# Stacked score products, q and k one step ahead, and row-wise sums of squares in a two-layer hybrid encoder

## The chip, the cores and the metric

The kernel runs on one core of one Trainium2 chip. The metric is the device time of one execution in microseconds (us), as the median of several runs. A profiled execution gives the trace from which every row below comes; its own time and its span (first to last instruction) stand in the table further down.

## The reference, cut to what matters

Two layers with 512 tokens of width 1024. In each layer one projection of x feeds three branches: a bidirectional state-space scan (SSD), a differential attention with rotary positions, and a cross-attention into 256 memory tokens. Sigmoid gates merge the branches, an output projection and a layer norm follow. The change lies in the differential attention:

```python
q = _apply_rope(dq.reshape(Bsz, S, 8, 2, 64), cos, sin)     # 8 heads, 2 maps each, 64 wide
k = _apply_rope(dk.reshape(Bsz, S, 8, 2, 64), cos, sin)
s = einsum('bqhcd,bkhcd->bhcqk', q, k) * 64 ** -0.5
p = softmax(s)
w = p[:, :, 0] - lam * p[:, :, 1]
o = einsum('bhqk,bkhe->bqhe', w, v)
o = _rmsnorm(o, diff_norm_w) * (1 - lambda_init)           # over the 128 columns of a head
y_diff = o * silu(dg)
```

Everything is float32 at the boundary.

## The kernel before, in words

**Precision.** Nearly all products are made of single-pass float32r matmuls on a high part and a low part. `split(h, l, x)` (L93) writes the high part with ScalarE and the rest with VectorE; `mm3` (L105) adds the products low*high, high*low and high*high in one PSUM bank. A few products are plain float32, among them the transposes and the heads' sums of squares.

**Weights and units.** `emit` (L131) runs through a plan of jobs. Each unit of weights (128x1024, 512 KB) is loaded into `wr` by SyncE's queue (two buffers), split into `wh` and `wl` (three buffers each), two units ahead of its use. All DMAs of the kernel are issued on SyncE's queue, in one order. A projection of one unit (`proj`, `proj2`) is 24 matmuls of 512 columns into a bank of the pool `pj` (three banks).

**Order.** The program's scheduler orders each engine's instructions by priority and by its own estimate of times; in the differential attention TensorE's order is written by hand (`manual_schedule`), and other work may be put between. Pools: `pm` four PSUM banks (scores, values), `pt` a single bank (transposes, sums), `pj` three.

**The differential attention (`diff`).** A step (L966) is one unit's projection in two halves, with jobs ahead of the first half and between the halves. For head h the units are `rope(h + 1, "q")`, `rope(h + 1, "k")` and two of gates' or values' parts, so a head takes four steps and the 32 query blocks of 128 rows are numbered s = 0 to 31. `rope` (L819) takes the projection to SBUF (`rx`), lets four small DMAs swap its 32-row groups into `rsw`, multiplies by cosine and sine, and splits the sum into two tiles `q0`, `q1` (or `k0`, `k1`). The head's first map lies in partitions 0 to 63, the second in 64 to 127. Step s issues `scores(s + 1)` first; between the halves come `values` (on even steps) and `turn(s)`, the transposes of a block's weights. `scores` (L873) makes six matmuls of 64 rows, maps alternating, into two banks:

```python
for n, (a, b) in enumerate(((ql, kh), (qh, kl), (qh, kh))):
    for c in range(2):
        rows = slice(64 * c, 64 * c + 64)
        self.mm(pss[c], a[rows, qs], b[rows, :], n == 0, n == 2)
```

then for each map a minimum (`fmx`, VectorE) and an exponential (`fpp`, ScalarE). `values(h, 1)` (L907) squares the head's output into a tile `fth`; `sums(h)` (L921), one step later, contracts it with a column of ones, four float32 products of one column each into `pt`, and ScalarE copies 128x4 numbers to `ss`. `norm` (L927) turns `ss` into the heads' factors, in a chain of small VectorE operations: once for heads 0 to 6 behind step 29, once for head 7 behind step 33. For the first seven heads `spread` transposes the factors, stores them, and `fin(h)` loads them broadcast; for head 7 `last` spreads them with TensorE in step 34. `fin(h)` multiplies and splits into the tiles `dy0`, `dy1`, from which the branch's output projection starts.

**Ahead gates.** `AHEAD` (L40) names gate projections that are made between the parts of the SSD, stored to DRAM and loaded again where they are used; the keys are (group, part) of the SSD, the values (branch, row of 128 columns). The gates of branch 1 that are not ahead are the last units of the differential attention.

Of the kernel before, what the change touches and what calls it, by code (L numbers as in the profile page):

```python
# [15 lines left out]
ALU = mybir.AluOpType  # L16
# [16 lines left out]

PCW, PCB, PNW, PGB, PDN, PLG, PLB, PDS, NP_ = 0, 120, 144, 160, 184, 185, 193, 201, 217

CID, CTF, CTB, CON, CMK, CINV, CSG, NCST = 0, 128, 256, 384, 512, 768, 769, 770

AHEAD = {(0, 1): [(2, 0)], (0, 2): [(2, 1)], (0, 3): [(2, 2)], (1, 0): [(2, 3)], (1, 2): [(2, 4)],  # L40
         (2, 0): [(2, 5)], (2, 2): [(2, 6)], (3, 0): [(2, 7)], (3, 2): [(1, 0)]}

# [7 lines left out]
def bc(ap, shape):  # L52
    return ap.broadcast_to(shape)


class Net:
# [736 lines left out]
    def diff(self, l):  # L793
# [3 lines left out]
        def begin():  # L797
            self.df_ctx = ExitStack()
            fp = self.fp = self.df_ctx.enter_context(self.tc.tile_pool(name="diffp", bufs=2, reuse_waits="tile"))
            self.dy = [self.t(fp, [P, KC, S], f"dy{i}", F32R, bufs=1) for i in range(2)]  # L800
            lt = self.t(fp, [P, S], "ro", bufs=1)
            lq = lt[:, :256].rearrange("p (i e) -> p i e", i=4)
            nc.sync.dma_start(out=lq, in_=self.a["lam"][l:l + 1].broadcast_to([P, 4, 64]))
            lp = lt[:, 256:384].rearrange("p (i e) -> p i e", i=2)
            lv = lq.rearrange("p (i j) e -> p i j e", j=2)
            self.tt(lp, lv[:, :, 0, :], lv[:, :, 1, :], ALU.mult)
            ls = self.t(fp, [P, 2], "ls", bufs=1)
            nc.vector.reduce_sum(out=ls, in_=lp, axis=AX.X)
            self.act(ls, ls, AF.Exp)
            self.nlam = self.t(fp, [P, 1], "nlam", bufs=1)  # L810
            self.tt(self.nlam, ls[:, 1:2], ls[:, 0:1], ALU.subtract)
            self.ts(self.nlam, self.nlam, -lam0, ALU.add)
            self.dnw = self.t(fp, [P, 1], "dnw", bufs=1)
            self.ts(self.dnw, self.par[:, PDN:PDN + 1], 0.5 * (1.0 - lam0), ALU.mult)
            self.qk, self.v = {}, {}
            self.sdy = self.t(fp, [P, KC, S], "sdy", bufs=1)
            self.s0, self.ss = (self.t(fp, [P, 4 * KC], f"fs{i}", bufs=1) for i in range(2))

        def rope(h, nm):  # L819
            def f(wh, wl):  # L820
                fp = self.fp
                ps = yield from self.proj2(wh, wl)
                x = self.t(fp, [P, S], "rx")

                self.act(x, ps, scale=-0.125 if nm == "q" else 1.0)
                sw = self.t(fp, [P, S], "rsw")
                for i in range(4):
                    nc.sync.dma_start(out=sw[32 * i:32 * i + 32], in_=x[32 * (i ^ 1):32 * (i ^ 1) + 32])
                self.tt(x, x, self.cos, ALU.mult)
                self.tt(sw, sw, self.sin, ALU.mult)  # L830
                self.tt(x, x, sw, ALU.add)

                self.qk[h, nm] = [self.t(fp, [P, S], f"{nm}{i}", F32R) for i in range(2)]
                self.split(*self.qk[h, nm], x)
            return f, (l, (UQ if nm == "q" else UK) + h)

        def vpart(h):
# [35 lines left out]
        def scores(s):  # L873
            h, qc = divmod(s, 4)
            fp = self.fp
            (qh, ql), (kh, kl) = self.qk[h, "q"], self.qk[h, "k"]
            qs = slice(qc * P, (qc + 1) * P)
            mx = self.t(fp, [P, 2], "fmx")
            sm = self.t(fp, [P, 2], "fsm")
            pp = self.pp[s] = self.t(fp, [P, 2, S], "fpp")  # L880
            s0 = self.s0[:, s:s + 1]

            pss = [self.bank(self.pm, "pm") for _ in range(2)]
            for n, (a, b) in enumerate(((ql, kh), (qh, kl), (qh, kh))):
                for c in range(2):
                    rows = slice(64 * c, 64 * c + 64)
                    self.mm(pss[c], a[rows, qs], b[rows, :], n == 0, n == 2)
            for c, ps in enumerate(pss):
                nc.vector.tensor_reduce(out=mx[:, c:c + 1], in_=ps, axis=AX.X, op=ALU.min)  # L889
                self.act(pp[:, c, :], ps, AF.Exp, scale=-1.0, bias=mx[:, c:c + 1],  # L890
                         accum_out=s0 if c == 0 else sm[:, 1:2])

            nc.vector.reciprocal(out=sm[:, 1:2], in_=sm[:, 1:2])
            self.ts(sm[:, 1:2], sm[:, 1:2], s0, ALU.mult, self.nlam, ALU.mult)
            self.stt(pp[:, 0, :], pp[:, 1, :], sm[:, 1:2], pp[:, 0, :], ALU.mult, ALU.add)
# [11 lines left out]
        def values(h, qp):  # L907
            if qp == 0:
                self.po = self.bank(self.pm, "pm")
            po, wT, v = self.po, self.wT, self.v[h]  # L910
            for kc in range(4):
                e = slice(kc * P, (kc + 1) * P)
                self.mm3(po[:, 2 * qp * P:2 * (qp + 1) * P], v[0][:, e], v[1][:, e],
                         wT[0][:, kc, :], wT[1][:, kc, :], kc == 0, kc == 3)
            if qp:
                self.sq = self.t(self.fp, [P, S], "fth")
                self.act(self.sq, po, AF.Square)
                y = self.sdy[:, h, :]
                self.stt(y, po, self.dnw, y, ALU.mult, ALU.mult)

        def sums(h):  # L921
            pt = self.bank(self.pt, "pt")
            for c in range(4):
                self.mm(pt[:, c:c + 1], self.sq[:, c * P:(c + 1) * P], self.ones[:, 0:1])
            self.act(self.ss[:, 4 * h:4 * h + 4], pt[:, 0:4])

        def norm(lo, hi):  # L927

# [19 lines left out]
        def last():  # L948

            r = self.r  # L950
            self.rb = self.bank(self.pm, "pm")
            for c in range(4):
                self.mm(self.rb[:, c * P:(c + 1) * P], bc(r[:, c:c + 1], [P, P]), self.ident)

        def fin(h):
            y = self.sdy[:, h, :]
# [27 lines left out]
        self.T(lambda: order.enter_context(self.tc.manual_schedule(engines={mybir.EngineType.PE})))  # L984
        step(rope(0, "q"), (), ())
        step(rope(0, "k"), (), ())
        step(vpart(0), (), ())
        step(vpart(1), (), (job(scores, 0),))
        units = []
        for h in range(KC):  # L990
            if h + 1 < KC:
                units += [rope(h + 1, "q"), rope(h + 1, "k")]
                units += [gpart(h), gpart(h + 1)] if h % 2 == 0 else [vpart(h + 1), vpart(h + 2)]
        gates = [j for j in range(KC) if (1, j) not in self.ahead_gates]
        units += [gate(j) for j in gates]
        nst = 4 * KC
        for s, unit in enumerate(units):
            first = [job(scores, s + 1)] if s + 1 < nst else []
            amid = []
            if s % 4 == 2 and s < nst:  # L1000
                amid.append(job(values, s // 4, 0))
            if s % 4 == 0 and 0 < s <= nst:
                amid.append(job(values, s // 4 - 1, 1))
            if s < nst:
                amid.append(job(turn, s))
            if s % 4 == 1 and 1 < s <= nst + 1:
                first.append(job(sums, s // 4 - 1))
            if s == nst - 2:
                amid.append(spread)
            if s == nst + 2:  # L1010
                amid.append(last)
            step(unit, first, amid)
            if s in (nst - 3, nst + 1):
                self.T(job(norm, *((0, KC - 1) if s < nst else (KC - 1, KC))))
            for h in {nst: (0, 1), nst + 1: (2, 3, 4), nst + 2: (5, 6, 7)}.get(s, ()):
                self.T(job(fin, h))
        self.T(order.close)
# [18 lines left out]
    def wout(self, l, load, fill):  # L1036
# [3 lines left out]
        def begin():  # L1040
            op = self.op = self.fp
            self.rT = self.t(op, [P, 4, D], "dy0", bufs=1)
            if last:
                gb = self.t(op, [P, 4, D], "dy1", bufs=1)
                self.gb = [gb[:, i, :] for i in range(4)]
                nc.sync.dma_start(out=gb[:, 2:, :], in_=self.a["lngb"][l - 1:l].broadcast_to([P, 2, D]))
                nc.sync.dma_start(out=gb[:, :2, :], in_=self.a["lngb"][l:l + 1].broadcast_to([P, 2, D]))
            else:
                load(op, "dy1", "rsw", "q0")
            self.st = self.t(op, [P, S], "ro", bufs=1)[:, :48].rearrange("p (c i e) -> p c i e", c=4, i=2)  # L1050

        def resid(p, c):

            r = self.t(self.op, [P, S], (("q1", "rx"), ("k0", "k1"))[p][c // 2])
            src = self.a["x"] if l == 0 else self.nd
            e = slice(p * S, (p + 1) * S)
            nc.sync.dma_start(out=r, in_=src[c * P:(c + 1) * P, e])
# [111 lines left out]
def pack(x, mem, positions, w_in, conv_w, conv_b, dt_bias, a_log, d_skip, ssd_norm_w, diff_lam, diff_norm_w,  # L1169
# [33 lines left out]
    cst[:, CON:CON + P] = 1.0  # L1203
    cst[:, CMK:CMK + P] = np.where(ar[:, None] <= ar[None, :], 0.0, -1e30)
    cst[:, CMK + P:CMK + 2 * P] = np.where(ar[:, None] >= ar[None, :], 0.0, -1e30)
    cst[:, CINV] = inv[ar % 32]
    cst[:, CSG] = np.where(ar % 64 < 32, -1.0, 1.0)
    return {
# [26 lines left out]
```

## Time and profile before

| | |
|---|---|
| median of 3 runs | 2222.38 us (2219.97 to 2222.85) |
| the profiled execution's own time | 2223.68 us |
| its span | 2221.9 us |
| granted TensorE clock, mean | 0.997 |
| layer 0, attention proper (steps 0 to 30) | about 735 to 985 us |
| layer 1, the same | about 1840 to 2090 us |

A row of the timeline has the start in us from the span's start, the time it lasted, the engine, the line of the code, the operation, the tiles written and read, the shape and the count, and in brackets the engine's idle time before it and what ended that. Matmuls overlap in the pipeline, so what one costs is read from the distance between starts, not from its duration. A row of windows gives the stretch, its length, the busy time and count of PE, PEld (weight loads), DVE (VectorE), ACT (ScalarE) and POOL (GpSimd), the granted clock, the share of the DMA engines and GB/s.

### The profile page before, as it was taken

Reading aid. Unit: us, or ns where it says so; the run is one execution under the profiler, and the core shown is the slowest. Engines: PE = TensorE matmul, PEld = TensorE weight load, DVE = VectorE, ACT = ScalarE, POOL = GpSimd, SP = SyncE. Lnnn points to the kernel's source line nnn. Section 1 sums busy time; section 2 is a strip of 40 time slices with the busy share of each in tenths; the row PEclk is TensorE's granted clock in tenths of the full one; section 3 lists DMA queues with packets and bytes.
Section 4 is the critical chain, followed back from the end, with each engine's and each line's share of the span. In section 5 each row is a group of like instructions: output and inputs, shape, how many; then the busy total and the mean of one; then the engine's idle time right before and its main releaser. Section 6 shows DMA issues by size and latency. Waiting matters only on the chain.

```text
span 2221.9 us, 29523 instructions
## 1 busy us (share of the span) xinstructions
PE 2171.0 (98%) x11330; PEld 1768.0 (80%) x11330; DVE 1585.9 (71%) x2440; ACT 1004.3 (45%) x1895; POOL 54.2 (2%) x38
## 2 busy tenths in 40 slices
PE   8999999999999999999999999999999999999998
PEld 6787877788887888878887777777788887888786
DVE  7887878758554777766467888888754547777567
ACT  5664545424442454543355564545423324554440
POOL 0000000000000000000000100000100000000000
PEclk9999999999999999999999999999999999999999
DMA  4654554425553322224564654454434333222353
GB/s 149 182 160 144 144 136 144 125 86 167 168 173 117 95 85 79 77 89 147 152 214 122 177 146 145 133 152 132 124 105 132 105 113 94 75 84 81 91 154 112
DMA packets 106162, 283.73 MB, mean 128 GB/s; under 512 B 12524, under 2 KB 13092, under 8 KB 105764
## 3 DMA queue, kind: packets, MB, share of 16 engines
q1 hardware_dynamic: 106020, 281.84, 42.4%
q8 instruction: 89, 1.46, 0.3%
q14 instruction: 53, 0.43, 0.1%
HBM read 255.55 MB, written 17.85 MB: 123 GB/s over the span
## 4 chain that ended last, share of the span: by engine, by line
PE 71%; DVE 14%; DMA 8%; ACT 5%; issue 1%; POOL 0%; SPq 0%; POOLq 0%; DVEq 0%; ACTq 0%
PE pj L103 55%; PE pm L103 13%; DMA ab<-dab 5%; DVE wl L81 3%; PE pt L111 2%; DVE ab L81 2%; DVE acc L84 2%; ACT ab L91 1%; ACT wh L91 1%; DMA wr<-wu 1%; DVE y L81 1%; DVE rx L81 1%; PE pt L103 1%; DMA fth<-rd 1%; DVE m L81 1%
## 5 line engine op out<-in xcount | busy, mean ns | idle before, releaser
L103 PE MATMUL pj<-xh,wl 128*128 128x512 f32 x1664 | 669.2, 402 | 11.0 <-DVE wl L81 8.9
L103 PE MATMUL pj<-xh,wh 128*128 128x512 f32 x1664 | 661.0, 397 | 0.0
L103 PE MATMUL pj<-xl,wh 128*128 128x512 f32 x1664 | 658.5, 396 | 0.0
L81 DVE TENSOR_TENSOR wl<-wr,wh 128x1024 fp32r<-128x1024 f32 x330 | 405.7, 1230 | 109.0 <-ACT wh L91 108.1
L91 ACT ACTIVATE wh<-wr 128x1024 fp32r<-128x1024 f32 x330 | 347.4, 1053 | 228.4 <-PE pj L103 147.4
L103 PEld LDWEIGHTS pj<-xh,wl 128*128 128x128 f32 x1664 | 313.9, 189 | 91.2 <-issue 18.3
L103 PEld LDWEIGHTS pj<-xh,wh 128*128 128x128 f32 x1664 | 313.8, 189 | 71.7 <-issue 5.7
L103 PEld LDWEIGHTS pj<-xl,wh 128*128 128x128 f32 x1664 | 314.2, 189 | 63.6 <-issue 3.6
L91 ACT ACTIVATE ab<-ab,bias 128x128 f32<-128x128 f32 x512 | 160.8, 391 | 120.5 <-DVE ab L81 119.7
L84 DVE SCALAR_TENSOR_TENSOR acc<-pj,hcw,acc 128x510 f32<-128x510 f32 x192 | 142.4, 744 | 24.2 <-ACT acc L91 22.8
L91 ACT ACTIVATE fpp<-pm,fmx 128x512 f32<-128x512 f32 x128 | 87.9, 687 | 84.3 <-DVE fmx L889 83.6
L889 DVE TENSOR_REDUCE fmx<-pm 128x1 f32<-128x512 f32 x128 | 87.0, 686 | 45.9 <-PE pm L103 45.5
L103 PE MATMUL pj<-yl,wh 128*128 128x512 f32 x256 | 102.4, 400 | 0.9 <-DVE yl L84 0.9
L103 PE MATMUL pj<-yh,wh 128*128 128x512 f32 x256 | 103.0, 403 | 0.0
L81 DVE TENSOR_TENSOR ab<-ab,cst 128x1024 f32<-128x1024 f32 x64 | 85.4, 1334 | 24.4 <-DMA ab<-dab 24.4
L103 PE MATMUL pj<-dy,wh 128*128 128x512 f32 (+1 forms) x384 | 102.2, 354 | 0.1
L103 PE MATMUL pj<-yh,wl 128*128 128x512 f32 x256 | 102.0, 399 | 0.0
L103 PE MATMUL pj<-cy,wh 128*128 128x512 f32 x256 | 78.8, 389 | 0.0
L103 PEld LDWEIGHTS pj<-dy,wh 128*128 128x128 f32 x384 | 67.8, 189 | 11.0 <-DVE dy L81 0.9
L103 PE MATMUL pj<-wh,xl 128*128 128x256 f32 x256 | 74.8, 292 | 0.0
L81 POOL TENSOR_TENSOR sqa<-sqa,sz 128x512 f32<-128x512 f32 x32 | 52.9, 1654 | 845.6 <-ACT sz L91 845.6
L103 PE MATMUL pj<-wl,xh 128*128 128x256 f32 x256 | 72.4, 283 | 0.0
(273 smaller groups left out, 3269.1 us busy)
## 6 DMA issues: line engine op xcount, KB each, us to landing
wr<-wu SPq DMA_DIRECT2D x336, 512.0 KB, 3.7
ab<-dab SPq DMA_DIRECT2D x64, 512.0 KB, 5.7
eb<-deb SPq DMA_DIRECT2D x64, 256.0 KB, 4.7
mkv<-dkv SPq DMA_DIRECT2D x16, 512.0 KB, 4.5
rsw<-rx SPq DMA_DIRECT2D x128, 64.0 KB, 2.0
dgt<-tg SPq DMA_DIRECT2D x18, 256.0 KB, 2.8
dkv<-mo SPq DMA_DIRECT2D x16, 256.0 KB, 4.2
dkv<-q SPq DMA_DIRECT2D x16, 256.0 KB, 3.6
```

The source lines that it names most:

```text
L81: (eng or self.nc.vector).tensor_tensor(out=out, in0=a, in1=b, op=op)
L84: self.nc.vector.scalar_tensor_tensor(out=out, in0=a, scalar=s, in1=b, op0=op0, op1=op1)
L91: self.nc.scalar.activation(out=out, in_=a, func=f, **kw)
L103: self.nc.tensor.matmul(out=out, lhsT=a, rhs=b, start=first, stop=last)
L111: self.nc.tensor.transpose(out=out, in_=x, identity=self.ident)
L889: nc.vector.tensor_reduce(out=mx[:, c:c + 1], in_=ps, axis=AX.X, op=ALU.min)
```

## The change

Each map's k is stacked as 128 rows, high part over low part, and each map's q as 128 rows with the high part twice and the low part twice. A block's scores are then two matmuls of 128 rows for each map. The stacking is done by DMA: `rope` splits into a tile `qkh` and issues four copies between SBUF partitions. The stacked q of two heads lies in the storage that `dy0` has later. The unit order is changed: q of head h + 2 comes behind head h's other units, k of head h + 1 comes first, and `rope(1, "q")` moves ahead of the value parts. The squared output is split too (`sqs`, in the storage of `dy1`); `sums(h)` multiplies it by `pick`, a matrix whose column h is one, so a head's sums are row h of an 8x512 result, and the rows of all heads are added up in `sr`. `flip` turns `sr` back to 128 rows with four transposes ahead of each `norm`. `room` takes the two `dy` tiles at the end of step 32. The gate (1, 0) is no longer made ahead, (2, 7) is made one part later. Some tiles of the output projection change their storage.

```diff
 AHEAD = {(0, 1): [(2, 0)], (0, 2): [(2, 1)], (0, 3): [(2, 2)], (1, 0): [(2, 3)], (1, 2): [(2, 4)],
-         (2, 0): [(2, 5)], (2, 2): [(2, 6)], (3, 0): [(2, 7)], (3, 2): [(1, 0)]}
+         (2, 0): [(2, 5)], (2, 2): [(2, 6)], (3, 1): [(2, 7)]}
...
-            self.dy = [self.t(fp, [P, KC, S], f"dy{i}", F32R, bufs=1) for i in range(2)]
-            lt = self.t(fp, [P, S], "ro", bufs=1)
+            self.qst = self.t(fp, [P, KC, S], "dy0", F32R, bufs=1)
+            lt = self.t(fp, [P, S], "fth")
...
+            sx = self.t(fp, [P, KC, S], "dy1", F32R, bufs=1)
+            self.sqs = [sx[:, 2 * i:2 * i + 2, :] for i in range(2)]
+            self.sr = self.t(fp, [KC, S], "sr", bufs=1)
+            self.pick = self.t(fp, [P, KC, KC], "pick", F32R, bufs=1)
+            self.act(self.pick, self.cst[:, CPK:CPK + KC * KC].rearrange("p (h i) -> p h i", h=KC))
...
-                self.qk[h, nm] = [self.t(fp, [P, S], f"{nm}{i}", F32R) for i in range(2)]
-                self.split(*self.qk[h, nm], x)
+                hl = self.t(fp, [P, 2, S], "qkh", F32R)
+                self.split(hl[:, 0, :], hl[:, 1, :], x)
+                half = [slice(64 * c, 64 * c + 64) for c in range(2)]
+                if nm == "q":
+                    o = [self.qst[:, 4 * (h % 2) + 2 * c:4 * (h % 2) + 2 * c + 2, :] for c in range(2)]
+                    self.qk[h, nm] = [[t[:, i, :] for i in range(2)] for t in o]
+                    parts = [(o[c][r], hl[half[c]]) for c in range(2) for r in half]
+                else:
+                    o = self.qk[h, nm] = [self.t(fp, [P, S], f"k{c}", F32R) for c in range(2)]
+                    parts = [(o[c][half[i], :], hl[half[c], i, :]) for c in range(2) for i in range(2)]
+                for to, src in parts:
+                    nc.sync.dma_start(out=to.bitcast(F32), in_=src.bitcast(F32))
...
-            for n, (a, b) in enumerate(((ql, kh), (qh, kl), (qh, kh))):
-                for c in range(2):
-                    rows = slice(64 * c, 64 * c + 64)
-                    self.mm(pss[c], a[rows, qs], b[rows, :], n == 0, n == 2)
+            for c in range(2):
+                (qh, ql), k = self.qk[h, "q"][c], self.qk[h, "k"][c]
+                self.mm(pss[c], ql[:, qs], k, True, False)
+                self.mm(pss[c], qh[:, qs], k, False, True)
...
-                self.sq = self.t(self.fp, [P, S], "fth")
-                self.act(self.sq, po, AF.Square)
+                sq = self.t(self.fp, [P, S], "fth")
+                self.act(sq, po, AF.Square)
+                self.sq = [self.sqs[h % 2][:, i, :] for i in range(2)]
+                self.split(*self.sq, sq)
...
         def sums(h):
             pt = self.bank(self.pt, "pt")
+            for i in (1, 0):
+                self.mm(pt[:KC], self.pick[:, h, :], self.sq[i], i == 1, i == 0)
+            if h == 0:
+                self.act(self.sr, pt[:KC])
+            else:
+                self.tt(self.sr, self.sr, pt[:KC], ALU.add)
+
+        def flip(lo, hi):
+
+            pt = self.bank(self.pt, "pt")
             for c in range(4):
-                self.mm(pt[:, c:c + 1], self.sq[:, c * P:(c + 1) * P], self.ones[:, 0:1])
-            self.act(self.ss[:, 4 * h:4 * h + 4], pt[:, 0:4])
+                nc.tensor.transpose(out=pt[:, c * KC:(c + 1) * KC], in_=self.sr[:, c * P:(c + 1) * P],
+                                    identity=self.ident[:KC, :KC])
+            self.act(self.ss[:, 4 * lo:4 * hi].rearrange("p (h c) -> p h c", c=4),
+                     pt[:, :4 * KC].rearrange("p (c h) -> p h c", c=4)[:, lo:hi])
...
+        def room():
+            self.dy = [self.t(self.fp, [P, KC, S], f"dy{i}", F32R, bufs=1) for i in range(2)]
...
         step(rope(0, "q"), (), ())
         step(rope(0, "k"), (), ())
+        step(rope(1, "q"), (), ())
         step(vpart(0), (), ())
         step(vpart(1), (), (job(scores, 0),))
         units = []
         for h in range(KC):
             if h + 1 < KC:
-                units += [rope(h + 1, "q"), rope(h + 1, "k")]
+                units.append(rope(h + 1, "k"))
                 units += [gpart(h), gpart(h + 1)] if h % 2 == 0 else [vpart(h + 1), vpart(h + 2)]
+            if h + 2 < KC:
+                units.append(rope(h + 2, "q"))
...
             if s in (nst - 3, nst + 1):
+                self.T(job(flip, *((0, KC - 1) if s < nst else (KC - 1, KC))))
                 self.T(job(norm, *((0, KC - 1) if s < nst else (KC - 1, KC))))
+            if s == nst:
+                self.T(room)
...
-                load(op, "dy1", "rsw", "q0")
-            self.st = self.t(op, [P, S], "ro", bufs=1)[:, :48].rearrange("p (c i e) -> p c i e", c=4, i=2)
+                load(op, "dy1", "rsw", "qkh")
+            self.st = self.t(op, [P, 48], "st", bufs=1).rearrange("p (c i e) -> p c i e", c=4, i=2)
...
-            r = self.t(self.op, [P, S], (("q1", "rx"), ("k0", "k1"))[p][c // 2])
+            r = self.t(self.op, [P, S], (("fth", "rx"), ("k0", "k1"))[p][c // 2])
...
+    cst[:, CPK:] = np.eye(KC).reshape(1, -1)
```

More of the change, by code (lines that the diff above doesn't have):

```diff
@@ L34 @@
 PCW, PCB, PNW, PGB, PDN, PLG, PLB, PDS, NP_ = 0, 120, 144, 160, 184, 185, 193, 201, 217
-CID, CTF, CTB, CON, CMK, CINV, CSG, NCST = 0, 128, 256, 384, 512, 768, 769, 770
+CID, CTF, CTB, CON, CMK, CINV, CSG, CPK, NCST = 0, 128, 256, 384, 512, 768, 769, 770, 834
 AHEAD = {(0, 1): [(2, 0)], (0, 2): [(2, 1)], (0, 3): [(2, 2)], (1, 0): [(2, 3)], (1, 2): [(2, 4)],
-         (2, 0): [(2, 5)], (2, 2): [(2, 6)], (3, 0): [(2, 7)], (3, 2): [(1, 0)]}
+         (2, 0): [(2, 5)], (2, 2): [(2, 6)], (3, 1): [(2, 7)]}
 LX, LD, LN = 70, 80, 300
@@ L875, in scores @@
             fp = self.fp
-            (qh, ql), (kh, kl) = self.qk[h, "q"], self.qk[h, "k"]
             qs = slice(qc * P, (qc + 1) * P)
```

## The prediction

> **What bounds the kernel now.** I read the page first, then the windows of the two attention stretches. A change of under 0.2% (4.4 us) can't be told from none here.
>
> ```profile
> span 2221.9 us, 29523 instructions
> PE 2171.0 (98%) x11330; PEld 1768.0 (80%) x11330; DVE 1585.9 (71%) x2440; ACT 1004.3 (45%) x1895; POOL 54.2 (2%) x38
> ...
> 735.00:985.00 250.00, 248.34 (x1434) 199.87 (x1433) 183.72 (x322) 126.98 (x255) 0.00 (x0) 1.00 0.29 84
> 1840.00:2090.00 250.00, 248.30 (x1435) 199.98 (x1432) 184.11 (x322) 126.64 (x255) 0.00 (x0) 1.00 0.29 84
> ```
>
> TensorE is busy for 248 of 250 us in both attention stretches, VectorE for 184, ScalarE for 127, the DMA engines for 29%. The clock is full. So time goes or comes with what TensorE must do and wait for. Since a matmul's duration hides how far it overlaps the next, I read the distances between starts in the timeline of TensorE, here around an ordinary score block:
>
> ```profile
> 818.28 0.39 PE L103 MATMUL pj<-xh,wh 128*128 128x512 f32 x1
> 818.60 0.96 PE L103 MATMUL pm<-k,q 64*128 64x512 f32 x6
> 819.49 0.50 PE L103 MATMUL pj<-xh,wl 128*128 128x512 f32 x1
> 819.83 0.39 PE L103 MATMUL pj<-xl,wh 128*128 128x512 f32 x1
> 820.06 0.40 PE L103 MATMUL pj<-xh,wh 128*128 128x512 f32 x1
> ```
>
> A full matmul of 128 rows and 512 columns starts 0.23 us after the one before (819.83 to 820.06). The block costs 819.83 - 818.28 - 2 * 0.23 = 1.09 us: 0.89 for its six matmuls of 64 rows (818.60 to 819.49), and 0.09 and 0.11 more than 0.23 at the way in and out.
>
> The first block of a head is dearer, since its k is not ready:
>
> ```profile
> 826.79 0.39 PE L103 MATMUL pj<-xh,wh 128*128 128x512 f32 x1
> 827.21 0.51 PE L103 MATMUL pm<-k,q 64*128 64x512 f32 x2
> 827.94 0.73 PE L103 MATMUL pm<-k,q 64*128 64x512 f32 x4 [0.22 <-DVE k L81]
> ...
> 828.95 0.40 PE L103 MATMUL pj<-xl,wh 128*128 128x512 f32 x1
> ```
> ```profile
> 794.13 0.29 PE L103 MATMUL pj<-wl,xh 128*128 128x256 f32 x1
> 794.25 0.28 PE L103 MATMUL pj<-wh,xh 128*128 128x256 f32 x1
> ...
> 795.13 0.73 PE L103 MATMUL pm<-k,q 64*128 64x512 f32 x4 [0.16 <-DVE k L81]
> ...
> 796.01 0.28 PE L103 MATMUL pj<-wl,xh 128*128 128x256 f32 x1
> ```
>
> That is 828.95 - 826.79 - 0.46 = 1.70 us ahead of an odd head, and 796.01 - 794.25 - 2 * 0.12 = 1.52 ahead of an even one (its neighbours are of 256 columns, 0.12 apart). In both, VectorE's low part of k comes late.
>
> The sums of squares follow one block of each head:
>
> ```profile
> 810.34 0.39 PE L103 MATMUL pj<-xh,wh 128*128 128x512 f32 x1
> 810.66 0.96 PE L103 MATMUL pm<-k,q 64*128 64x512 f32 x6
> 811.55 1.05 PE L103 MATMUL pt<-cst,fth 128*128 128x1 f32 x8
> ...
> 812.78 0.39 PE L103 MATMUL pj<-xl,wh 128*128 128x512 f32 x1
> ```
>
> Block and sums cost 812.78 - 810.34 - 0.46 = 1.98, the sums 0.89 of it.
>
> **The change part by part.** *Scores and sums on TensorE.* Per layer there are 18 ordinary blocks, 4 late ones of odd heads, 3 of even heads, 7 with sums, and head 7's sums alone: 18 * 1.09 + 4 * 1.70 + 3 * 1.52 + 7 * 1.98 + 0.89 = 45.7 us. After it there are 32 * 4 matmuls for scores and 8 * 2 for sums, each of 128 rows and 512 columns: 144 * 0.23 = 33.1 us. That is 12.6 us less a layer, 25.2 in all, of which 7.5 are waits that end (2 * (4 * 0.61 + 3 * 0.43)). The sums' result has only 8 rows; whether such a product needs a way in and out as the 64-row blocks do (0.2) no row shows. Ends 0 and 16 * 0.2 = 3.2; I take 1.6.
>
> Rule against it: the Trainium skill's TensorE: Matmul & The Clock Gate (Part 3: Packing small matmuls) says that products in different row groups run at once, a pack lasting one matmul plus about 4 ns per further tile. By that the six matmuls would last as three, 0.69 against 0.92 for the stacked four, and stacking would cost 64 * 0.23 = 14.7 us. The trace agrees only in part: the pairs do overlap, but three of them take 0.89.
>
> *Flips.* Four transposes, twice a layer. The rows of a block's transposes:
>
> ```profile
> 805.91 1.60 PE L103 MATMUL pm<-wT,v 128*128 128x256 f32 x12
> 807.35 0.60 PE L111 MATMUL pt<-cst,fpp 128*128 128x128 f32 x4
> 807.70 0.49 PE L103 MATMUL pj<-xh,wl 128*128 128x512 f32 x1
> 808.02 0.40 PE L103 MATMUL pj<-xl,wh 128*128 128x512 f32 x1
> ```
>
> 808.02 - 807.35 - 0.23 = 0.44 each, 1.8 in all. Ends 0.5 (four narrow loads all but hidden) and 4.
>
> *The squares' split and the adding up.* The squares come from `values`, which ends at 805.91 + 1.60 = 807.5; the sums start at 811.55. In these 4 us lie now a square, after it also a high part and a low part. By the rows of k's split just below, 0.63 and 0.69, the three take some 2 us: hidden, with 2 us to spare for ScalarE's and VectorE's other work. The adding up is one more VectorE instruction of 512 columns (about 0.69) in place of ScalarE's copy. VectorE gets 2 * 0.69 a head, 11 us a layer more, 195 in about 238: 82% busy instead of 74%. ScalarE gets 0.63 a head. Both I cost at nothing in steady state; without that cover, see the second rival.
>
> *Stacking by DMA.* The way of k in a head now, on ScalarE, SyncE's queue, VectorE, ScalarE and VectorE:
>
> ```profile
> 818.71 0.60 ACT L91 ACTIVATE rx<-pj 128x512 f32<-128x512 f32 x1 [2.16 <-PE pj L103]
> 819.33 2.41 SPq L828 DMA_DIRECT2D rsw<-rx  x4
> 825.81 0.69 DVE L81 TENSOR_TENSOR rx<-rx,rsw 128x512 f32<-128x512 f32 x1
> 826.53 0.63 ACT L91 ACTIVATE k<-rx 128x512 fp32r<-128x512 f32 x1 [1.50 <-DVE rx L81]
> 827.19 0.69 DVE L81 TENSOR_TENSOR k<-rx,k 128x512 fp32r<-128x512 f32 x1
> ```
> ```profile
> wr<-wu SPq DMA_DIRECT2D x336, 512.0 KB, 3.7
> rsw<-rx SPq DMA_DIRECT2D x128, 64.0 KB, 2.0
> ```
>
> From the copy's start to the low part's end it is 827.88 - 818.71 = 9.2 us. Four copies behind it are issued in 2.4 us (as the four swaps, 819.33 plus 2.41) and land 2.0 to 3.7 us after issue (64 and 512 KB; 128 KB is near 2.2): the last at 9.2 + 1.8 + 2.2 = 13.2. Before, k had one step; now two. Two steps were 827.21 - 810.66 = 16.6 us and lose 2 * 0.4: 15.8. So k is in time with 2.6 us to spare, q (three steps) with 10. SyncE's queue gets 8 more issues a head, 4.8 us beside 31. But it is served in order: q's four copies wait for q's split, and behind them stand the next unit's swaps and the weight load. q's unit now directly precedes k's, so its low part is ready 9.2 us after its start and k's swaps could go at 7.9; when the copies stand first, k's swaps go at 9.2 + 2.4, 3.7 late, 1.1 more than the spare. When the swaps stand first, nothing is late. I take 0.15 us for each of 14 heads, 2.0; ends 0 and 14 * 1.1 = 15. The weight loads have slack: one lands 3.7 us after issue and its split is used two units later.
>
> *Prologue.* One more unit (24 * 0.23 = 5.5 us) before the values; the same unit is missing later, so nothing is added. The first k needs 13.2 us; it gets two and a half units, 13.8. I take 0.5 a layer; ends 0 and 2.
>
> *The end of the attention.* Sums of the last head, their copy, the factor and its spreading:
>
> ```profile
> 1005.28 0.95 PE L103 MATMUL pt<-cst,fth 128*128 128x1 f32 x8
> ...
> 1017.35 1.16 PE L103 MATMUL pm<-cst,rs_y 128*128 128x128 f32 x8 [0.54 <-DVE rs_y L81]
> ```
> ```profile
> 1007.53 0.16 ACT L91 ACTIVATE fs<-pt 128x4 f32<-128x4 f32 x1
> ```
> ```profile
> 1017.14 0.16 DVE L81 TENSOR_TENSOR rs_y<-rs_y,fs 128x4 f32<-128x4 f32 x1
> ```
>
> The chain from sums to factor takes 9.6 us on VectorE, mixed with the other heads' products, and TensorE waits for it. `flip` stands behind the step's whole projection, so the sums reach `ss` at about 1005.3 + 0.5 + 5.5 + 0.44 + 0.4 = 1012.1, 4.4 us later. Then the other heads' products are mostly done and the chain is quicker: a dozen ops of 0.16 with a gap each are 2.5 us at least. Factor ready between 1014.6 and 1021.7, against 1017.3; nearer the middle, I take 1.5 us later. TensorE fills part with projections from the `dy` tiles, as now. The first flip delays `spread` in the same way:
>
> ```profile
> 989.58 0.28 PE L111 MATMUL pt<-cst,rs_y 128*28 128x128 f32 x1 [1.41 <-DVE wT L81]
> ```
>
> It waits already for the bank, so of some 4 us lateness I take 1. Together 2.5 a layer, 5.0; ends -2 and 17 (both flips' whole lateness). `room` ties `dy1` to head 7's sums, so the first products of `fin` may not start before 1005.8; the first now runs at about that time.
>
> *The SSD's end.* A gate's 5.5 us of TensorE move from the SSD into the attention, with its store and load gone. There VectorE is the tighter one:
>
> ```profile
> 420.00:440.00 20.00, 20.00 (x123) 16.62 (x122) 18.23 (x26) 11.03 (x26) 2.62 (x2) 1.00 0.65 200
> ```
> ```profile
> 453.29 1.05 PE L103 MATMUL pt<-cst,sqa 128*128 128x1 f32 x8 [1.21 <-POOL sqa L81]
> ```
>
> VectorE is busy for 18.2 of 20, and TensorE waits at the stage's end already. If it arrives earlier it may wait longer, at most 5.5 a layer; but the gates behind can be pulled ahead, and VectorE has one weight split less. Ends -2 and 11 in all; I take 0, since other gates stand ready.
>
> *Sum.* 25.2 - 1.6 - 1.8 - 2.0 - 1.0 - 5.0 = 13.8 us less. From the profiled execution's 2223.7 (span 2221.9) that is 2209.9; the median of the runs lies 1.3 lower, so 2208.6.
>
> **The rivals.** *k comes late (slower).* Place: the first block of 14 heads. If SyncE's order puts q's copies ahead of k's swaps, k is 1.1 us late, and each microsecond by which busier VectorE stretches the 9.2 adds to it. For: the queue is in order and the copies wait. Against: 2.6 us to spare and a scheduler that places DMAs by readiness. It decides from about (13.8 + 2.0) / 14 = 1.1 us of wait a head; at 2.2 us the time is 2222.4 - 15.8 + 14 * 2.2 = 2237.
>
> *The sums hold the single `pt` bank (no change).* The next transposes start 12 * 0.23 = 2.8 us behind the sums and need the bank read out. VectorE has two minima, a weight split and the adding up in that place, 3 * 0.69 and the 128x1024 row's
>
> ```profile
> L81 DVE TENSOR_TENSOR wl<-wr,wh 128x1024 fp32r<-128x1024 f32 x330 | 405.7, 1230 | 109.0 <-ACT wh L91 108.1
> ```
>
> 1.23: 3.3 us against 2.8 plus the 0.5 of the sums. If TensorE waits 0.8 us in 14 steps, 11 us are lost: 2220.
>
> *The packing was worth more.* If three overlapped pairs were worth three pitches, 0.69, and the rest of a block's time went on elsewhere, the stacked four at 0.92 would cost 64 * 0.23 = 14.7 us more. With the ended waits' 7.5 and the sums' 16 * 0.43 = 6.9 saved and the delays of 11.4 the time is 2222.4 + 11.7 = 2234. Against: 0.89 between starts. This is what the Trainium skill's rule above would make of it.
>
> *The delays don't come.* Flips and heads wait for nothing: 25.2 - 3.4 = 21.8 less, 2201.
>
> **How the numbers follow.** Forecast 0.57 (2202 to 2218), no delays 0.15, the bank 0.12 (a quarter of it still faster), k late 0.14, packing 0.02. Faster 0.57 + 0.15 + 0.03 = 0.75; same 0.09 of the bank and 0.02 of a k only a little late, 0.11; slower 0.12 of late k and 0.02 of packing, 0.14. The range runs from 2196 (no delays and a gain at the SSD's end) to 2226; late k of over 1.4 us a head lies outside.
>
> **What would show it.** Score blocks: four matmuls of 128 rows 0.23 apart, 0.92 from first to next. No wait for k at a head's first block (else: the first rival, with a DMA named as releaser). Sums: two starts 0.23 apart, no idle before the next `fpp` transposes. Flip: some 0.4 us. The `last` products: idle of 1 to 3 us. The prediction would be wrong if the queue's order starves k or the weight loads, if VectorE at 82% delays the transposes, or if the SSD's end opens a gap.

## The result: slower by 1.7%, for the wait that was given one chance in seven

The changed kernel takes 2257.18 us (median of 4 runs, 2252.85 to 2260.99) against 2221.18 for the kernel before (2217.34 to 2222.85): a ratio of 1.0166, 95% interval 1.0152 to 1.0180. Forecast were 2208.6 and a range that ended at 2226. The profiled execution took 2256.38 us, its span is 2254.6. From the page of the changed kernel, the span, the engines' busy times and the group of the score products:

```profile
span 2254.6 us, 29437 instructions
PE 2170.7 (96%) x11122; PEld 1779.2 (79%) x11122; DVE 1605.6 (71%) x2470; ACT 1008.7 (45%) x1903; POOL 53.1 (2%) x38
...
L103 PE MATMUL pm<-k,dy 128*128 128x512 f32 x256 | 76.5, 415 | 33.3 <-DMA k<-qkh 32.7
```

The last row says by itself what happened: TensorE stood idle for 33.3 us ahead of the score products, and 32.7 of these ended when a copy of k (`k<-qkh`) landed. (`dy` in it is the storage of the stacked q.) The windows of the attention say the same; before, TensorE was busy for 248 of 250 us there:

```profile
740.00:990.00 250.00, 232.98 (x1264) 195.13 (x1263) 179.55 (x304) 120.94 (x241) 0.00 (x0) 0.99 0.46 121
1860.00:2110.00 250.00, 233.30 (x1263) 194.90 (x1262) 180.01 (x303) 120.17 (x239) 0.00 (x0) 0.99 0.46 121
```

TensorE now idles for 17 of 250 us. VectorE has not become fuller (180 busy, 184 before, both in 250), and the DMA engines' share went from 0.29 to 0.46. The spans by stage, as differences between the starts of TensorE's and ScalarE's instructions that mark them; the last column is an experiment told below:

| stage (layer 0 / layer 1, us) | before | changed | whole change, k in time |
|---|---|---|---|
| up to the attention's first projection | 721.2 / 672.6 | 716.9 / 665.6 | 718.0 / 670.7 |
| from there to the first scores | 14.0 / 14.0 | 20.3 / 20.0 | 19.3 / 19.3 |
| first to last scores | 247.8 / 247.7 | 262.4 / 262.1 | 236.9 / 236.9 |
| last scores to the layer's output projection | 80.0 / 80.4 | 81.3 / 81.7 | 81.6 / 81.8 |
| the rest of the layer | 90.0 / 54.2 | 90.0 / 54.4 | 90.0 / 54.5 |

The span grew by 32.7 us (2254.6 - 2221.9; that the waits for k come to the same figure is chance), and 29 of these lie between first and last scores. The first two rows belong together: the gate that left the SSD and the unit that moved ahead of the values. Now a first block of a head in the changed kernel, and an ordinary block, in TensorE's timeline:

```profile
870.68 0.28 PE L103 MATMUL pj<-wh,xh 128*128 128x256 f32 x1
872.99 1.31 PE L103 MATMUL pm<-k,dy 128*128 128x512 f32 x4 [2.03 <-DMA k<-qkh]
874.13 0.39 PE L103 MATMUL pj<-xh,wl 128*128 128x512 f32 x1
874.36 0.40 PE L103 MATMUL pj<-xl,wh 128*128 128x512 f32 x1
```
```profile
879.86 0.39 PE L103 MATMUL pj<-xh,wh 128*128 128x512 f32 x1
880.09 1.10 PE L103 MATMUL pm<-k,dy 128*128 128x512 f32 x4
881.02 0.39 PE L103 MATMUL pj<-xh,wl 128*128 128x512 f32 x1
881.25 0.40 PE L103 MATMUL pj<-xl,wh 128*128 128x512 f32 x1
```

The ordinary block costs 881.25 - 879.86 - 2 * 0.23 = 0.93, as forecast (0.92). The first one costs 874.36 - 870.68 - 0.12 - 0.23 = 3.33: 2.03 of waiting, and later starts around it. Added up over all 66 places by this reading, scores and sums cost 92.2 us before and 113.6 after; without waits the 66 would cost about 67.

Why k lands late stands in the timeline of SyncE's queue. k's unit was taken from PSUM at 854.65 (on ScalarE, `rx`):

```profile
855.25 1.14 SPq L836 DMA_DIRECT2D rsw<-rx  x2
856.50 3.18 SPq L853 DMA_DIRECT2D dy<-qkh  x4
859.73 2.63 SPq L836 DMA_DIRECT2D rsw<-rx  x2
862.46 2.69 SPq L138 DMA_DIRECT2D wr<-wu  x2
869.26 2.43 SPq L853 DMA_DIRECT2D k<-qkh  x4
```

q's four copies, 256 KB each, were issued between the second and the third of k's four swaps (`rsw<-rx`). The landings, from the same trace: the swaps at 857.15 (the first) and 864.96 (the last), q's copies at 859.48, 861.37, 862.69 and 864.53, k's last copy at 873.46. The page's list of issues has the sizes and the median times to landing:

```profile
dy<-qkh SPq DMA_DIRECT2D x64, 256.0 KB, 4.5
...
rsw<-rx SPq DMA_DIRECT2D x128, 64.0 KB, 2.0
k<-qkh SPq DMA_DIRECT2D x64, 128.0 KB, 2.3
```

Two things happened to the last swap. It was issued at 861.14 instead of some 857.1 (855.25 and three issues of 0.6), so 4.0 us late, and landed 3.8 us after issue instead of 2.0. (In the heads from the third on, where the trace shows it, the last swap took 2.9 to 4.7 us to land.) So k's way from copy to last landing is 873.46 - 854.65 = 18.8 us, where the prediction had 13.2 and 15.8 to spend. Two theories were open on this: the queue and its bytes, or VectorE, which also had new work in those steps. And within the first: is it the place in the issue order, or the 1 MB that moves?

### The profile page after: what moved, and what is told of

Read it like the earlier page. It is cut to its first block, busy times and chain, and to the rows that moved or that the text cites. A ratio compares the mean times of both kernels' runs of the same rounds, so it can differ in the third digit from the quotient of the medians.

```text
span 2254.6 us, 29437 instructions
## 1 busy us (share of the span) xinstructions
PE 2170.7 (96%) x11122; PEld 1779.2 (79%) x11122; DVE 1605.6 (71%) x2470; ACT 1008.7 (45%) x1903; POOL 53.1 (2%) x38
## 3 DMA queue, kind: packets, MB, share of 16 engines
q8 instruction: 87, 1.43, 0.3%
## 5 line engine op out<-in xcount | busy, mean ns | idle before, releaser
L103 PE MATMUL pm<-k,dy 128*128 128x512 f32 x256 | 76.5, 415 | 33.3 <-DMA k<-qkh 32.7
L103 PEld LDWEIGHTS pm<-k,dy 128*128 128x128 f32 x256 | 45.9, 192 | 51.0 <-issue 30.5
```

The source lines that it names most:

```text
L103: self.nc.tensor.matmul(out=out, lhsT=a, rhs=b, start=first, stop=last)
```

## The experiments

Ratios are to the kernel before, measured in the same call, with 95% intervals.

**q's copies on another queue.** The changed kernel, with

```diff
-                    nc.sync.dma_start(out=to.bitcast(F32), in_=src.bitcast(F32))
+                    (nc.gpsimd if nm == "q" else nc.sync).dma_start(out=to.bitcast(F32), in_=src.bitcast(F32))
```

> The changed kernel with one edit: q's four stacking copies are issued on GpSimd's queue, everything else on SyncE's as before. Same bytes, same VectorE work, same TensorE work. Theory A (queue): q's copies of 256 KB each stand between the second and the third of the next k's swaps in SyncE's queue; k's way is 4 to 5 us longer for it, and TensorE waits 2.0 to 3.3 us at the first block of every head. Taken off that queue, k's swaps land within about 4 us of k's projection, the waits for k fall below 0.5 us a head, and the time falls by about 2 * 20 us to 2213 to 2220. Theory B (VectorE): k is late because VectorE has more to do in its way; then the queue does not matter, the waits stay near 2 us and the time within 0.3% of 2257. Theory C (DMA bytes): the copies' bytes slow every transfer, whichever queue; then the swaps still take 3.8 us instead of 2.0 to land, waits fall by half at most, 2235 to 2250.

2219.23 us, ratio 1.0007 (0.9997 to 1.0017). The changed kernel stood 36.0 us above the kernel before, this one 0.9: 35 us back by the queue alone. The group of score products on its page:

```profile
L103 PE MATMUL pm<-k,dy 128*128 128x512 f32 x256 | 71.3, 399 | 4.7 <-DMA k<-qkh 4.6
```

The wait falls from 33.3 to 4.7 us with VectorE's work unchanged, so the queue is the cause and VectorE's work by itself is not. In a head at 844 us of this trace the second to last and the last swap, though issued without delay, still landed 3.4 and 5.1 us after issue instead of 2.0: q's 1 MB is under way beside them. The Trainium skill (DMA: Bandwidth & Descriptors, section Issuing engines are not separate DMA queues) says that copies issued from different engines run on the same 16 DMA engines and interleave; these landings agree.

**q's unit one step earlier.** The changed kernel, with

```diff
-                units.append(rope(h + 2, "q"))
+                units.insert(-1, rope(h + 2, "q"))
```

so that a unit of gates or values lies between q's and k's.

> The changed kernel with one edit: in every head q's unit stands third instead of fourth, so one other unit lies between it and the next k's. All DMAs stay on SyncE's queue. Theory A: q's copies are issued before k's swaps want to go, all four swaps go together, waits for k under 0.5 us a head, 2213 to 2222. Theory B: VectorE's work is the same and only moved, waits stay, about 2250 to 2257. Theory C: the bytes are the same but spread; between the two, 2230 to 2245.

2216.09 us, ratio 0.9991 (0.9979 to 1.0003). The wait ahead of the score products is 6.3 us in all, nearly all of it at the first blocks of heads 0 and 1. Both ways to keep q's copies out from among k's swaps end the loss; neither makes the kernel clearly faster than before.

**q's copies cut to an eighth.** The changed kernel, with the four copies at their place but of 64 of 512 columns (32 KB each); seven eighths of the stacked q are left out:

```diff
+                if nm == "q":
+                    parts = [(to[:, :, :64], src[:, :, :64]) for to, src in parts]
```

> The changed kernel with q's four stacking copies cut to 64 of 512 columns each (32 KB instead of 256 KB); they keep their number and their place in SyncE's queue, between k's second and third swap. Left out: seven eighths of the stacked q, which stays at a value written once at the stage's start, so the scores are others. Theory A1 (issue order): the swaps wait for q's split and four issues, 2.4 us and more, whatever the bytes; TensorE still waits 1.5 us or more for k at each head, 2240 to 2255. Theory A2 (bytes): the four copies' 1 MB keeps the DMA engines busy for some 6 us and the swaps behind it land late; with 128 KB the swaps are late by the issues alone, which the 2.6 us to spare covers: waits under 0.5 us, 2212 to 2222.

2219.65 us, ratio 0.9996 (0.9987 to 1.0004).

```profile
L103 PE MATMUL pm<-k,dy 128*128 128x512 f32 x256 | 71.0, 398 | 2.4 <-DMA k<-qkh 1.6
```

The issues stand as before between the swaps (in a head at 844 us: two swaps, four copies from 845.39 to 848.08, two swaps at 848.13 and 848.77), so k's last swap still goes 2.8 us late. But it lands 2.7 us after issue (in most other heads 2.0), and the wait is 2.4 us in all. So the place in the order alone nearly fits into the spare time (2.6 us in the prediction), and so do the bytes alone, in the experiment with the other queue. It takes both, the place and the 1 MB, to make k late at every head.

**The order alone.** The kernel before, with the new order of units, the prologue's extra unit and the moved gate; scores and sums as before.

```diff
+         step(rope(1, "q"), (), ())
...
-                units += [rope(h + 1, "q"), rope(h + 1, "k")]
+                units.append(rope(h + 1, "k"))
...
+            if h + 2 < KC:
+                units.append(rope(h + 2, "q"))
```

> The kernel before with the change's order of units and its ahead gates alone: k one step ahead, q three, one unit more in the prologue, gate (1, 0) in the attention. Scores in 64-row pairs and the sums as before, no stacking copies. Theory A: nothing new stands in the queue, the waits for k at 14 first blocks (0.43 to 0.61 us each, 7.5 in all) go, the rest is moved work: 2213 to 2217 against 2221. A rival (order): moving the gate and the prologue's unit opens gaps of its own at the SSD's end or at the first scores, and the time does not fall: 2220 to 2230.

2214.06 us, ratio 0.9982 (0.9971 to 0.9993); from first to last scores it takes 4.0 us less a layer. In the view of the score products no idle time stands any more (before: 2.7 us, 13 times), and every block of the 50 without sums costs 1.09 to 1.10.

**The row sums alone.** The kernel before, with squares split, `pick`, `sr`, `flip` and `room`; scores, stacking and order as before.

```diff
+            for i in (1, 0):
+                self.mm(pt[:KC], self.pick[:, h, :], self.sq[i], i == 1, i == 0)
-            for c in range(4):
-                self.mm(pt[:, c:c + 1], self.sq[:, c * P:(c + 1) * P], self.ones[:, 0:1])
```

> The kernel before with the row sums alone (the split of the squares, two products of 512 columns, adding up, flip, room); scores, rope and order of units as before. The products save 16 * 0.43 = 6.9 us on TensorE. Theory A: the waits that the changed kernel shows at these products (0.3 us, for the transposes' bank) and the later factors at the end (about 1.3 us a layer net) take most of it back: 2216 to 2223. A rival (flips): both flips' whole lateness of some 4 us a layer lands on TensorE and the time rises: 2224 to 2230.

2224.94 us, ratio 1.0029 (1.0020 to 1.0039): a cheaper product (two row sums cost 0.47 where they stand alone in the changed kernel, the eight columns 0.91) and a slower kernel. Who waits, in the view of the score products of this kernel and then of the kernel before:

```profile
  ACT k L91: 9.4, 12
  DVE k L81: 3.2, 14
```
```profile
  DVE k L81: 2.3, 11
  ACT k L91: 0.4, 2
```

The wait for k grew from 2.7 to 12.6 us. In the head at 813 us, k's way takes 10.1 us (812.99 to 823.06) instead of 9.2, with VectorE's other work standing between its parts. So VectorE's and ScalarE's new work does delay k where k has one step of time. The time lies in the range of the rival, but not for its reason: what grew is the wait for k and not one for the flips.

**Stacking alone, and with half of q's copies off the queue.** The first is the changed kernel in the order of the second experiment, but with the old sums and `norm`, no `flip`. In the second, GpSimd also copies the two halves of q that stay on their partitions, and two DMAs of 256 KB remain:

```diff
+                if nm == "q":
+                    for c, r in enumerate(half):
+                        nc.gpsimd.tensor_copy(out=o[c][r], in_=hl[r])
+                    parts = [(o[c][half[1 - c]], hl[half[c]]) for c in range(2)]
```

> The changed kernel with q's unit third in a head and with the sums, their copy and the norms of the kernel before (no split of the squares, no row sums, no flip): stacked scores alone. From its relatives: q third alone gave 2216 with the row sums; the row sums alone cost 6 us in the kernel before. Theory A: scores 64 * (1.09 - 0.94) = 10 less and the waits for k of before gone (7.5), less the remaining waits for k: 2206 to 2212, below the order alone (2214). A rival (stacking gives nothing): a block's 0.15 us goes into new waits for k's copies, and it stands level with the order alone at 2212 to 2217.

> As the stacked scores alone, but the halves of q that stay on their partitions are copied by GpSimd, and only the two others by DMA: 512 KB instead of 1 MB a head, two issues instead of four. Theory A2 (bytes): k's swaps and weight loads land sooner, the waits for k that are left (2 us at the first head) shrink, 2204 to 2210, 1 to 4 us below the stacked scores alone. Theory A1 (issue order): nothing changes where q is already issued ahead of k's swaps, within 1.5 us of it. A rival: GpSimd's copies are late or slow down VectorE, and q itself comes late: 2212 and more.

2223.59 us (ratio 1.0011, 1.0003 to 1.0020) and 2219.44 (0.9990, 0.9981 to 0.9999). The first is above both ranges that were named for it. The second is above its forecast too, in the open range of its rival. First to last scores fell by 4.3 and 3.4 us a layer in the first, by 6.2 and 5.6 in the second; the order alone gave 4.0 of that. In the first, 6.2 us of idle time stay ahead of the score products. The rest of the difference lies outside the attention: the first's SSD of layer 1 is 3.6 us longer than in the order alone, and its two ends of the attention 2.7. Why the SSD, whose code is the same, comes out longer was not settled; two traces of the order alone differ there by 1.4 us themselves (666.9 and 668.3).

**All of it, with k in time.** The whole change with both mends (q one step earlier, two halves by GpSimd), beside the order alone and the stacking with own halves once more on one chip.

> The whole change (stacked scores, row sums, flips, new order) with both things that let k come in time: q's unit one step earlier and q's two staying halves copied on GpSimd, so two copies of 256 KB through SyncE's queue in place of four. If, with k in time, the stacked blocks (0.94 us against 1.09) and the row sums (some 0.5 us against 0.89) are worth on the clock what they are worth on TensorE, it is 64 * 0.15 + 16 * 0.4 = 16 us less, minus the 6 us that the row sums alone cost at k and at the flips, so some 10 us below the order alone in the same call: 2200 to 2208. Rival: what the attention gains is given back at the SSD and at the tail, as in the run with stacking alone: 2213 to 2220, no faster than the order alone.

> The order alone (q two heads ahead, the SSD's last gate moved into the attention), beside the two others of this call for comparison on one chip: 2213 to 2216, below the kernel before by 4 to 8 us. Rival: its gain in the earlier call was a chance of the chip: 2219 to 2222.

> Stacking with the old sums and q's staying halves copied on GpSimd, beside the order alone on one chip. If stacking brings something on top of the order: below the order alone, 2206 to 2212. Rival, as the earlier call's interval leaves it open: equal to the order alone or up to 5 us above it, 2214 to 2220.

2207.51 us, ratio 0.9939 (0.9926 to 0.9952); the order alone 2218.34, 0.9991 (0.9982 to 0.9999), a little above its expected 2213 to 2216; stacking with own halves 2218.65, 0.9988 (0.9977 to 1.0000), not to be told from the order alone. The whole change with k in time beats both kernels of this case, and the order alone too. From its page and its windows:

```profile
span 2208.8 us, 29462 instructions
PE 2157.7 (98%) x11122; PEld 1780.2 (81%) x11122; DVE 1607.7 (73%) x2470; ACT 1004.7 (45%) x1903; POOL 85.9 (4%) x70
```
```profile
740.00:970.00 230.00, 230.00 (x1284) 197.82 (x1283) 183.93 (x311) 121.48 (x247) 14.54 (x14) 1.00 0.44 117
1840.00:2070.00 230.00, 230.00 (x1279) 197.64 (x1278) 183.31 (x309) 121.27 (x246) 14.55 (x14) 1.00 0.44 117
```

TensorE is busy in 230 of 230 us. SyncE's queue and the first block of the same head as above:

```profile
836.30 1.14 SPq L857 DMA_DIRECT2D dy<-qkh  x2
841.74 2.44 SPq L836 DMA_DIRECT2D rsw<-rx  x4
844.28 0.53 SPq L138 DMA_DIRECT2D wr<-wu  x1
850.28 2.44 SPq L857 DMA_DIRECT2D k<-qkh  x4
```
```profile
856.61 0.39 PE L103 MATMUL pj<-xh,wh 128*128 128x512 f32 x1
856.83 1.10 PE L103 MATMUL pm<-k,dy 128*128 128x512 f32 x4
857.77 0.28 PE L103 MATMUL pj<-wh,xl 128*128 128x256 f32 x1
857.89 0.28 PE L103 MATMUL pj<-wl,xh 128*128 128x256 f32 x1
```

The four swaps stand together and land 2.0 us after issue each. k's way from the copy at 841.11 to its last landing at 854.44 is 13.3 us (13.2 in the prediction), and TensorE takes it up at 856.83, 2.4 us later, without a wait. Beside the kernel with q one step earlier alone, which was not faster than the kernel before, what is gone are the waits at heads 0 and 1: scores and sums fall from 78 to 67 us by the reading of the blocks.

Why stacking with own halves, which has the same two copies, gains less than this is seen in the same two views of its trace:

```profile
820.72 1.14 SPq L852 DMA_DIRECT2D k<-qkh  x2
821.95 0.54 SPq L138 DMA_DIRECT2D wr<-wu  x1
822.58 1.10 SPq L852 DMA_DIRECT2D k<-qkh  x2
```
```profile
827.68 1.22 PE L103 MATMUL pm<-k,dy 128*128 128x512 f32 x4 [0.73 <-issue]
```

Here a weight load of 512 KB was issued between k's second and third copy, and the third landed 5.0 us after issue instead of 2.3. Six heads pay about 1 us each: their first blocks cost 1.8 to 2.1 in place of 0.94. These six are exactly the heads in which a weight load stands among k's copies; in the other ten of this trace, and in all sixteen of the kernel with k in time, none does. It is the same fault with another big transfer in front. That this difference in the queue makes up the whole distance between the two kernels was not tried by itself; by the blocks, it is 6 us of 11, and the cheaper sums are 7 less what they cost at the end of the attention.

## Why the prediction was wrong

*The step that failed* is the term "k late", under stacking by DMA: 0.15 us for each of 14 heads, 2.0 in all, with 14 * 1.1 = 15 as its upper end. Measured, scores and sums cost 113.6 in the changed kernel and 67.3 in the one with k in time, 46.3 us apart. 39.4 of these are the first blocks of the 14 heads, 2.8 each, so the term was 39 us, 2.6 times its upper end. Another 3.1 lie at the first block of head 0, which the prediction had under the prologue, and 3.8 at the blocks with sums (below). All the other terms together hold within 3 us: forecast -15.8 without k, measured -13.1 in the whole change with k in time. Two parts of the step failed:

- The choice of order. The step named both orders and their result, q's copies ahead of k's swaps or behind them, and took the second with the argument that the scheduler places DMAs by readiness. The queue's rows show q's copies ahead of the third swap. q's low part was ready at 855.94, while the second swap was being issued (855.81 to 856.39). That the scheduler put the copies there for this reason is not shown, since its estimates are not on record.
- The price of the bad order. 1.1 us a head took only the wait for q's split and the time of four issues, 3.7 us less the 2.6 to spare. That delay was nearly right: in the head above the last swap is issued 4.0 us late. Not counted was that the swaps behind 1 MB also land late, here 3.8 us after issue instead of 2.0, 1.8 more; a part of the 4.0 is that the issues of the fourth copy and of the third swap are longer, 1.27 and 1.36 instead of 0.59. Together that is 5.8 us late, 3.2 beyond the spare time, against 2.8 a head on the mean. The landing of 2.0 was read off a row in which nothing big stood in front. The bounds were taken from undisturbed rows on both ends, and a term whose cause is a full queue has its upper end in the time of that queue's bytes: 8.0 us here, from the first issue of q's copies to their last landing. VectorE has no part in the difference in this head: it took k's first product 1.45 us after the last swap's landing (866.41 against 864.96), and 1.43 after it with k in time (847.04 against 845.61).

*The first rival* named mechanism, place and side, and the releaser to look for; its threshold of 1.1 us a head was passed: 39.4 / 14 = 2.8 on the mean. It had 0.14 and was priced at 2237 instead of 2257. The argument against it ("2.6 us to spare") had been worked out for the good order.

*Scores and sums on TensorE:* forecast 2 * 33.1 + 1.6 = 67.8, measured 67.3 with k in time; ordinary blocks 0.94 (0.92), block and sums 1.39 (1.38). Ahead of and behind the 8-row products there is no extra time; here the lower end held. A block with sums, in the kernel with k in time:

```profile
872.07 0.39 PE L103 MATMUL pj<-xh,wh 128*128 128x512 f32 x1
872.30 1.09 PE L103 MATMUL pm<-k,dy 128*128 128x512 f32 x4
873.23 0.62 PE L103 MATMUL pt<-dy,pick 128*8 128x512 f32 x2
873.68 0.39 PE L103 MATMUL pj<-xh,wl 128*128 128x512 f32 x1
873.91 0.40 PE L103 MATMUL pj<-xl,wh 128*128 128x512 f32 x1
```

873.91 - 872.07 - 2 * 0.23 = 1.38. The packing rule of the Trainium skill (TensorE: Matmul & The Clock Gate, Part 3), by which stacking would have lost 14.7 us, does not hold for these pairs: the stacked blocks are 0.15 cheaper, not 0.23 dearer.

*Flips:* forecast 0.44 each. In the changed kernel:

```profile
1027.57 0.39 PE L103 MATMUL pj<-xh,wh 128*128 128x512 f32 x1
1027.89 0.41 PE L953 MATMUL pt<-cst,sr 8*128 8x8 f32 x4
1028.23 0.50 PE L103 MATMUL pj<-xh,wl 128*128 128x512 f32 x1
1028.56 0.39 PE L103 MATMUL pj<-xl,wh 128*128 128x512 f32 x1
```

1028.56 - 1027.89 - 0.23 = 0.44 by the prediction's reading; with the way in, as the blocks are read, 1028.56 - 1027.57 - 0.46 = 0.53.

*The end of the attention:* forecast 2.5 a layer. In layer 0 `last` starts at 1037.32, 15.5 us behind the last head's sums (12.1 before), so it comes 3.4 later, where the prediction had 1.5; but 2.1 come back in the step after it, which leaves 1.3 a layer. *Prologue:* forecast 0.5 a layer beside the unit's 5.5; 0.8 and 0.5 in the changed kernel, with k in time -0.2. *The SSD's end:* forecast 0 with ends -2 and 11. A gate of 5.5 left; the stage became 4.3 and 7.0 shorter in the changed kernel, 3.2 and 1.9 in the other. Against the 11.0 that left, that is -0.3 and 5.9 us: within the ends, but the largest miss beside k. A part of the 5.9 is clock: the trace with k in time has four stretches of 3.4 us at half clock in its two SSDs (from 449.4, 527.9, 1275.5 and 1599.7), the kernel before two (from 454.3 and 1608.1), and a stretch costs TensorE at most half its length, 1.7 us. Two more of them are up to 3.4 us; the cause of the rest is open.

*The sums' bank* (second rival): not where it was put. The sums wait 0.13 to 0.18 us for the bank ahead of them, in six heads a layer, some 4 us in all with the later starts around it (23.3 against 19.4 for the 14 blocks with sums). It stays at 0.13 to 0.16 (once 0.64) where q's copies went to another queue, and is gone in both kernels with q one step earlier. So it came with the order of units; it belongs neither to late k nor to the sums.

So the forecast of 2208.6 was that of a kernel with another order in SyncE's queue. With k in time 2207.51 was measured, by terms that partly cancel: the SSD's end cost 5.9 more than forecast, the attention's end 2.0 less, k's 2.0 and the 1.6 of the 8-row products were not needed. That the two times come so close is partly luck.

## What to carry to other kernels

A small transfer on the critical way costs what stands ahead of it, in issues and in bytes: list, for the worst order that the queue may take, which big transfers are ready before it, and price the delay with their whole landing time. When only the good order fits into the spare time, make that order sure (another unit between, fewer bytes, another engine for the part that stays on its partitions) before counting any gain behind it. And parts of a change may not add up: the order alone gave 2 to 4 us, the row sums alone lost nearly 7, stacking over the order gave nothing, and all together with k in time gave 13.

## What the hardware showed beyond expectation

- A 64 KB swap behind four copies of 256 KB lands 3.8 us after issue instead of 2.0, and also from another queue's copies it suffers (3.4 and 5.1). A 128 KB copy behind a weight load of 512 KB takes 5.0 instead of 2.3.
- Issues grow longer behind q's copies: 1.36 and 1.22 us for the swaps and 1.27 for the fourth copy itself, where 0.59 is usual. With copies of an eighth the issues in these places take 0.59 to 0.60 (median over the heads).
- Waits can cost more than their length, by the granted clock (the column before the last two of a window's row). Behind a wait of 2.0 us at 766.04 and one of the same length at 838.66:

```profile
766.00:770.00 4.00, 3.96 (x10) 3.19 (x11) 2.53 (x5) 1.55 (x4) 0.00 (x0) 0.57 0.48 139
838.70:842.10 3.40, 3.40 (x14) 2.60 (x15) 2.39 (x5) 1.45 (x4) 0.00 (x0) 1.00 0.47 113
```

In the first the clock is 0.57 for 4 us, in the second it is full; in the changed kernel six such stretches stand, four of them at heads that wait for k; in the kernel before two, each behind a wait of 1.21 (453.29 and 1607.27). One more stands at the very end of each. The Trainium skill (TensorE: Matmul & The Clock Gate, Part 1) puts the low clock behind an idle window of about 3.4 us; here waits of 1.21 and 2.0 were enough, and others of 2.0 were not.
